# A two-block transformer stack in fp32: three edits at the start, at the bias rows and at the end

## The chip, the cores and the metric

The kernel runs on one core of one Trainium2 chip. The metric is device microseconds (us) of one execution; lower is better. The kernel before took 1858.72 us (median of 3 runs, 1858.06 to 1859.34).

## The reference

256 tokens of width 2048 go through two residual blocks and a norm, and then through a third block with two residual steps, all in fp32:

```
x = x + (mla(rmsnorm(x) @ w_in) * silu(gate)) @ w_out        # latent attention; c_q and c_kv are normed again
x = x + (swa(rmsnorm(x) @ w_in) * silu(gate)) @ w_out        # sliding window, 32 query heads
x = rmsnorm(x) * final_norm
proj = rmsnorm(x) @ w_in_2                                   # q, k, v of attention; z, xbc, dt of a state-space mixer
x = x + rmsnorm(concat(attn(q, k, v, rel_bias), ssm(z, xbc, dt)) @ w_out_2)
gate, up = split(causal_conv(rmsnorm(x) @ w_ffn_up))
x = x + rmsnorm((gelu(gate) * up) @ w_ffn_down)
```

The attention's relative bias depends on the head and on the distance of two tokens alone. In the latent attention `c_q` and `c_kv` (512 each) are columns of `rmsnorm(x) @ w_in` and get a norm of their own.

## The kernel before

Activations lie transposed: a tile `x` holds 128 features by 256 tokens, so the width is 16 tiles. The weights are a stream of some 600 pieces of 128 x 1024 fp32 (512 KB), in the order of use. `fetch` (L285 to 288) issues one on SyncE's queue (SP) into one of five buffers `raw`. `split_w` makes two halves of it: ScalarE copies it into the rounded type fp32r (`whi`, L304, told as L276 in the profile, since a helper records it), VectorE subtracts to get the rest (`wlo`, L305, told as L270); there are four buffers of each. Activations are split in the same way into one tile `hl` with the two halves side by side. In `proj` TensorE then multiplies `whi` by both halves (512 columns, L336) and `wlo` by the high half (256 columns, L339): one such pair per 128 features, eight pairs a piece, two pieces for one tile of 128 outputs in PSUM (`acc`). The two column halves of `acc` are added on the way out.

A scheduler sets the order of the instructions on each engine from its own estimate of their times; only parts marked `manual_schedule` keep the written order on the engines named there. All DMAs share eight completion lanes in rotation, so an engine that issues one can first have to wait for the one eight issues earlier. An engine that issues a DMA runs its instructions in order: what stands behind a waiting issue waits too.

The places that the change touches, in the order of the program:

- `start` (L652) issues the first loads on SP: x in groups of four tiles between half pieces of the first four weight pieces, and runs 14 small fp32 matmuls on a tile of ones (L662). `first_two` (L393) splits x times the layer's gain and the first four pieces in 256-column steps, in written order, and makes the first two output tiles side by side (L434, L437): 16 rows k, two accumulators each. Behind that the squares of x are summed for the first norm (`sq`, L421), and the norm `r1` is multiplied into each of the eight latent tiles `u` before their own norm.
- `out_mla` (L808) makes 16 output tiles with `proj`, two pieces each. At tile 8 it calls `biases` (L695): a matmul with a table of 0 and 1 spreads the relative bias over 384 distances for 8 heads, and one DMA on ScalarE's queue (L712) writes that row 128 times into DRAM (`biasrows`, 1536 KB), from where the attention later reads it skewed.
- `out_swa` (L906) makes 16 tiles and their norm; `mix` then begins with small preparations for the state-space part (L981 to 1000, L1013, L1032 to 1039): `wdts`, a 16-column weight in both halves, the exponential `ea`, scaled convolution weights, zeroed pads. The first matmuls of that stage (L351) multiply all 16 activations by `wdts`.
- `ffn` (L1213): the down projection turns the operands round, so that its outputs have 128 tokens by 512 columns. It has two passes `p` of 1024 outputs, 44 pieces each, and four accumulators (token half t, column half c). Token half 1 runs behind half 0 by `lag` pieces, and in the last pass its last four pieces are held to the end (`held`, L1268). Then come the final norm and the output, on VectorE in written order (L1310 to 1325): squares on ScalarE (`end`), the gain (`gain`), the sum and root, and eight outputs of 128 x 512, each with its DMA.

Of the kernel before, what the change touches and what calls it, by code (L numbers as in the profile page):

```python
# [40 lines left out]


class _Lazy:


    def __init__(self, n, make):
        self.n, self.make, self.made = n, make, {}

    def __len__(self):
        return self.n  # L50

    def __getitem__(self, k):
        if k not in self.made:
            self.made[k] = self.make(k)
        return self.made[k]
# [156 lines left out]

def _host(inputs):
    i = {n: np.asarray(a) for n, a in inputs.items()}
    return {
        "xt": np.ascontiguousarray(i["x"][0].T.reshape(KT, 128, S).transpose(1, 0, 2)),
# [11 lines left out]
class _Kernel:  # L228
    def __init__(self, ctx, tc, xt, pos, wst, wdt, vec, cst, rel, gfpost, out, dbg=None):
# [11 lines left out]
        self.raw = []  # L241
# [33 lines left out]
    def act(self, out, in_, func=AF.Copy, **kw):  # L275
        self.nc.scalar.activation(out, in_, func, **kw)  # L276
# [13 lines left out]
    def weights(self, pool=None):  # L290
        if not self.raw:
            self.fetch()
        self.piece += 1
        return self.split_w(self.raw.pop(0), HALF, pool)
# [98 lines left out]
    def first_two(self, xs, P):  # L393


        ws = []
        for i in range(4):
            self.piece += 1
            ws.append([self.wpool.tile([128, HALF], F32R, name=n, bufs=4) for n in ("whi", "wlo")])
        raw, self.raw = self.raw[:4], self.raw[4:]  # L400
        E = mybir.EngineType
        with self.tc.manual_schedule(engines={E.Activation, E.DVE}):
            for g in range(4):
                for k in range(4 * g, 4 * g + (2 if g == 0 else 4)):
                    xs[k]
                for i in (g // 2, 2 + g // 2):
                    hi, lo = ws[i]
                    for a in range(512 * (g % 2), 512 * (g % 2) + 512, 256):
                        w = slice(a, a + 256)
                        self.act(hi[:, w], raw[i][:, w])  # L410
                        self.tt(lo[:, w], raw[i][:, w], hi[:, w].bitcast(F32), ALU.subtract)
                if g == 0:
                    xs[2], xs[3]
            accs = self.columns(xs, ws)
            sums = []
            for x in self.x0:
                for a in (0, 2):
                    t = P.tile([128, 2, S], F32, name="sq2", bufs=4)
                    self.act(t, x[:, a : a + 2, :], AF.Square)
# [3 lines left out]
            t = sums[0]  # L423
            self.tt(t[:, 0, :], t[:, 0, :], t[:, 1, :], ALU.add)
# [78 lines left out]
    def rstd(self, c, n, out=None):  # L503
# [4 lines left out]
        self.act(r, c, AF.Sqrt, scale=1.0 / n, bias=self.eps)  # L508
        v.tensor_scalar(x, c, 1.0 / n, EPS, op0=ALU.mult, op1=ALU.add)
# [142 lines left out]
    def start(self):  # L652
# [4 lines left out]
        g1 = P.tile([128, KT], F32, name="g1")  # L657
        nc.scalar.dma_start(out=g1, in_=self.vec_dram[:, 0:KT])
        self.act(self.tmp("n0", (128, 2), 4), self.ones[:, 0:2])
        warm = self.aux.tile([128, 512], F32, name="s", bufs=2)  # L660
        for i in range(14):
            nc.tensor.matmul(warm[:, :128], self.ones, self.ones, start=True, stop=True)  # L662

        x4 = [P.tile([128, 4, S], F32, name="x0", bufs=4) for _ in range(4)]
        x0 = [t[:, j, :] for t in x4 for j in range(4)]
        self.raw = [self.new_raw() for _ in range(4)]
        self.fetched = 4
        for g in range(4):
            for a in (0, 2) if g == 0 else (0,):
                b = a + 2 if g == 0 else 4  # L670
                nc.sync.dma_start(out=x4[g][:, a:b, :], in_=self.xt[:, 4 * g + a : 4 * g + b, :])
                if a == 0:
                    w = slice(512 * (g % 2), 512 * (g % 2) + 512)
                    for i in (g // 2, 2 + g // 2):
                        nc.sync.dma_start(out=self.raw[i][:, w], in_=self.wst[i, :, w])
# [3 lines left out]
        self.x0 = x4  # L679
        self.xs = _Lazy(KT, lambda k: self.split(self.hx, 16, x0[k], g1[:, k : k + 1]))  # L680
# [14 lines left out]
    def biases(self, P):  # L695
# [5 lines left out]
        nc.scalar.dma_start(out=hot, in_=self.cst_dram[0:33, at : at + n])  # L701
        rel = P.tile([33, 8], F32, name="rel")
        nc.vector.memset(rel, NEG)
        nc.scalar.dma_start(out=rel[0:32, :], in_=self.rel)
# [5 lines left out]
        nc.scalar.dma_start(out=self.wdt, in_=self.wdt_dram)  # L710
        self.bias = self.tc.dram_tile([128, 8, n], F32, name="biasrows")
        nc.scalar.dma_start(out=self.bias.rearrange("i h n -> h i n"),  # L712
                            in_=row.unsqueeze(1).to_broadcast([8, 128, n]))

    def mla(self):
# [5 lines left out]
        with self.pool("latent", side="right") as P:  # L721
            lat = []
            with self.pool("squares") as Q:
                accs, t = self.first_two(xs, Q)
                self.r1 = self.spread(self.rstd(self.mean(t[:, 0, :]), D))
            for name, gain in (("q", "gq"), ("kv", "gkv")):
                hl, ss = [], None
                for j in range(4):
                    u = self.both(accs.pop(0) if accs else self.proj(xs))
                    self.tt(u, u, self.r1, ALU.mult)  # L730
# [3 lines left out]
                self.rstd(self.mean(ss), 512, c)  # L734
# [73 lines left out]
    def out_mla(self):  # L808
# [3 lines left out]
        with self.pool("again") as P:  # L812
            for j in range(KT):
                if j == 8:
                    self.biases(P)
                if j == KT - 1:
                    self.roots(self.x[-2])
                if j % 4 == 0:
                    x0 = P.tile([128, 4, S], F32, name="x0", bufs=2)
                    nc.sync.dma_start(out=x0, in_=self.xt[:, j : j + 4, :])  # L820
# [85 lines left out]
    def out_swa(self):  # L906
# [3 lines left out]
        old, self.x, self.xs, ss, sg = self.x, [], [], None, None  # L910
        for j in range(KT):
# [452 lines left out]
```

## Time and profile before

| | |
|---|---|
| median of 3 runs | 1858.72 us |
| profiled execution, its span | 1858.8 us, 1857.0 us |
| TensorE matmul busy | 1828.4 us, 98% |
| VectorE, ScalarE busy | 1398.4 us (75%), 1030.2 us (55%) |
| weight stream | 320.49 MB, 50.4% of the time of 16 DMA engines |

The span is the time from the first to the last instruction that the hardware profiler recorded; the 1.8 us around it are launch and end. A busy TensorE is one that has a matmul in flight; matmuls overlap by some 0.1 to 0.15 us, so distances between starts tell more than durations. A gap is shown as an idle time with the instruction whose end released it.

### The profile page before, as it was taken

The numbers are of one execution on the slowest core, as the hardware profiler recorded it, in microseconds if no ns is written. First come the engines' busy times: TensorE is split into PE (matmuls) and PEld (weight loads), VectorE is DVE, ScalarE is ACT, GpSimd is POOL, SyncE is SP. The second block draws the span as 40 slices with busy tenths as digits, with TensorE's granted clock in tenths as the row PEclk, the third lists the DMA queues.
The fourth block names the chain that finished last, engine by engine and source line by source line (L and its number), as shares of the span: only waits on it lengthen the run. The fifth ranks groups of instructions, "written<-read, shape, count | busy, mean of one in ns | idle before, by whom it ended". The sixth has DMA issues, their size and how long they took to land.

```text
span 1857.0 us, 27806 instructions
## 1 busy us (share of the span) xinstructions
PE 1828.4 (98%) x10306; PEld 1572.9 (85%) x10306; DVE 1398.4 (75%) x2578; ACT 1030.2 (55%) x1832; POOL 0.2 (0%) x4
## 2 busy tenths in 40 slices
PE   9999999999999999999999989999999999999997
PEld 8999987898888887888888878888888888888886
DVE  8887776787888677977766578888888888855554
ACT  8655554567777655556554565444444444544543
POOL 0000000000000000000000000000000000000000
PEclk9999999999999999999999999999999999999999
DMA  8544456654444454544454645555555555555553
GB/s 291 176 151 157 148 175 184 215 183 150 144 158 150 158 191 138 182 170 152 149 194 140 206 145 174 181 182 190 184 187 188 184 191 182 196 186 187 202 187 120
DMA packets 92556, 326.13 MB, mean 176 GB/s; under 512 B 10339, under 2 KB 12804, under 8 KB 92420
## 3 DMA queue, kind: packets, MB, share of 16 engines
q1 hardware_dynamic: 89568, 320.49, 50.4%
q10 hardware_dynamic: 2852, 3.86, 1.1%
q8 instruction: 81, 1.33, 0.3%
q14 instruction: 55, 0.45, 0.1%
HBM read 320.64 MB, written 3.67 MB: 175 GB/s over the span
## 4 chain that ended last, share of the span: by engine, by line
PE 94%; DMA 2%; DVE 2%; ACT 1%; issue 1%; SPq 0%; DVEq 0%; ACTq 0%
PE acc L336 44%; PE acc L339 23%; PE acc L1264 4%; PE acc L1265 4%; PE acc L1266 4%; DMA biasrows<-bias 2%; PE acc L469 1%; PE acc L470 1%; PE acc L468 1%; PE m L594 1%; PE acc L450 1%; PE acc L451 1%; PE acc L449 1%; PE m L582 1%; PE s L791 1%
## 5 line engine op out<-in xcount | busy, mean ns | idle before, releaser
L336 PE MATMUL acc<-hl,whi 128*128 128x512 f32 x3584 | 1279.3, 398 | 4.1 <-ACT whi L276 4.1
L339 PE MATMUL acc<-hl,wlo 128*128 128x256 f32 x3584 | 1016.5, 284 | 3.7 <-DVE wlo L270 3.7
L276 ACT ACTIVATE whi<-raw 128x1024 fp32r<-128x1024 f32 (+1 forms) x606 | 628.6, 1041 | 670.3 <-PE acc L336 311.8
L270 DVE TENSOR_TENSOR wlo<-raw,whi 128x1024 fp32r<-128x1024 f32 (+1 forms) x606 | 727.0, 1203 | 352.5 <-ACT whi L276 348.8
L336 PEld LDWEIGHTS acc<-hl,whi 128*128 128x128 f32 x3584 | 674.1, 188 | 161.0 <-ACT whi L276 6.0
L339 PEld LDWEIGHTS acc<-hl,wlo 128*128 128x128 f32 x3584 | 673.8, 188 | 11.8 <-DVE wlo L270 5.2
L1265 PE MATMUL acc<-wlo,hl 128*128 128x512 f32 x344 | 136.1, 397 | 0.0
L1266 PE MATMUL acc<-whi,hl 128*128 128x512 f32 x344 | 135.3, 394 | 0.0
L1264 PE MATMUL acc<-whi,hl 128*128 128x512 f32 x344 | 118.2, 396 | 0.0
L273 DVE SCALAR_TENSOR_TENSOR g<-pad,vec,g 128x256 f32<-128x256 f32 x176 | 84.2, 482 | 2.8
L1265 PEld LDWEIGHTS acc<-wlo,hl 128*128 128x128 f32 x344 | 64.7, 188 | 16.0
L1264 PEld LDWEIGHTS acc<-whi,hl 128*128 128x128 f32 x344 | 64.7, 188 | 15.6
L1266 PEld LDWEIGHTS acc<-whi,hl 128*128 128x128 f32 x344 | 64.7, 188 | 15.2
L270 DVE TENSOR_TENSOR u<-acc,u 128x256 f32<-128x256 f32 x182 | 75.7, 418 | 0.4
L276 ACT ACTIVATE u<-acc 128x256 f32<-128x256 f32 x184 | 67.2, 366 | 5.7 <-DVE q L270 2.8
L276 ACT ACTIVATE t<-t,nm 128x128 f32<-128x128 f32 x112 | 49.4, 444 | 2.3 <-DVE nm L545 1.4
L270 DVE TENSOR_TENSOR t<-s,cst 128x384 f32<-128x384 f32 (+1 forms) x64 | 32.8, 520 | 20.0 <-PE s L890 12.8
L469 PE MATMUL acc<-wlo,hl 128*128 128x512 f32 (+1 forms) x128 | 47.1, 368 | 0.0
L470 PE MATMUL acc<-whi,hl 128*128 128x512 f32 (+1 forms) x128 | 47.1, 368 | 0.0
L468 PE MATMUL acc<-whi,hl 128*128 128x512 f32 (+1 forms) x128 | 46.8, 368 | 0.0
L451 PE MATMUL acc<-hl,wlo 128*128 128x256 f32 x160 | 45.7, 285 | 0.0
L449 PE MATMUL acc<-hl,whi 128*128 128x256 f32 x160 | 45.5, 284 | 0.0
(294 smaller groups left out, 1652.7 us busy)
## 6 DMA issues: line engine op xcount, KB each, us to landing
raw<-in_wst_dram SPq DMA_DIRECT2D x593, 512.0 KB, 3.3
x<-in_xt_dram SPq DMA_DIRECT2D x7, 512.0 KB, 6.0
raw<-in_wst_dram SPq DMA_DIRECT2D x8, 256.0 KB, 6.1
biasrows<-bias ACTq DMA_DIRECT2D x1, 1536.0 KB
b<-biasrows ACTq DMA_DIRECT2D x8, 128.0 KB, 2.8
gb<-in_gfpost_dram ACTq DMA_DIRECT2D x2, 512.0 KB, 4.7
out_dram<-f SPq DMA_DIRECT2D x4, 256.0 KB, 2.3
out_dram<-hl SPq DMA_DIRECT2D x4, 256.0 KB, 2.5
```

Source lines behind the costliest of these rows:

```text
L270: self.nc.vector.tensor_tensor(out=out, in0=a, in1=b, op=op)
L273: self.nc.vector.scalar_tensor_tensor(out=out, in0=a, scalar=s, in1=b, op0=op0, op1=op1)
L276: self.nc.scalar.activation(out, in_, func, **kw)
L336: nc.tensor.matmul(acc.rearrange("p a t -> p (a t)"), hi[:, a : a + 128], xs[k].rearrange("p a t -> p (a t)"), start=(k == 0), stop=False, ...
L339: nc.tensor.matmul(acc[:, 0, :], lo[:, a : a + 128], xs[k][:, 0, :], start=False, stop=(k == n - 1), skip_group_check=True)
L451: nc.tensor.matmul(acc[:, 0, :], lo[:, a : a + 128], x[:, 0, :], start=False, stop=(k == 3))
L468: nc.tensor.matmul(o, xh, hi[:, a : a + n], start=(k == 0), stop=False)
L469: nc.tensor.matmul(o, xh, lo[:, a : a + n], start=False, stop=False)
L470: nc.tensor.matmul(o, xl, hi[:, a : a + n], start=False, stop=(k == last))
L1264: nc.tensor.matmul(o, xh, hi[:, w], start=(k == 0), stop=False)
L1265: nc.tensor.matmul(o, xh, lo[:, w], start=False, stop=False)
L1266: nc.tensor.matmul(o, xl, hi[:, w], start=False, stop=(k == NF - 1))
```

## The change

Three edits are joined.

1. Start. x is stored with its gain in front (`_pack_x`), so that no separate load of the gain is needed. The first loads go out on two queues: four quarter pieces on ScalarE's, x and the rest on SP's. The first eight rows of the first two output tiles are computed as 16 plain fp32 matmuls of 256 columns, unsplit weights by x times gain (`xg`); the halves of these eight x, which later pieces need, are made by a VectorE copy and a GpSimd subtraction. Rows 8 to 15 go in halves as before, in 512-column steps. The halves of the next two pieces follow directly (`halved`), and the squares are released behind them (`issue_after(self.begun)`). Seven warm-up matmuls stand instead of 14. `r1` is no longer multiplied into the latent tiles, but into the mean of their squares (twice) and their norm (once).
2. Bias rows. `biases` runs at tile 3 and writes one row of 12 KB (`biasrow`); tiles 4 to 11 each issue one DMA inside DRAM that copies this row into 16 of the 128 rows.
3. The state-space preparations move into `out_swa` (`ssm_ready`, at tile 5). In the last pass of the down projection six pieces of token half 1 are held instead of four and come last in order; the end runs by token half: two gains, the sum of the first three squares with the epsilon, the root with the last square added in ScalarE's bias, four outputs; the output (t=1, q=2) goes out on ScalarE's queue.

```diff
@@ first_two
+        xg = [self.wpool.tile([128, 4, S], F32, name=n, bufs=4) for n in ("whi", "wlo")]
...
+        def halves(k):
+            v = xg[k // 4][:, k % 4, :]
+            nc.vector.tensor_copy(xs[k][:, 0, :], v)
+            nc.gpsimd.tensor_tensor(out=xs[k][:, 1, :], in0=v, in1=xs[k][:, 0, :].bitcast(F32),
+                                    op=ALU.subtract)
...
+            for g in range(2):
+                for k in range(4 * g, 4 * g + 4):
+                    self.act(xg[g][:, k % 4, :], x(k), scale=gain(k))
+                for k in range(4 * g, 4 * g + 4):
+                    halves(k)
+            for g in range(2):
+                w = slice(512 * g, 512 * g + 512)
+                for i in range(2):
+                    hi, lo = ws[i]
+                    self.act(hi[:, w], raw[2 * i + 1][:, w])
+                    self.tt(lo[:, w], raw[2 * i + 1][:, w], hi[:, w].bitcast(F32), ALU.subtract)
...
+            self.halved = [self.weights(), self.weights()]
+            self.begun = self.act(self.tmp("n5", (128, 1), 1), self.g1[:, 0:1]).ins
+        for k in range(KT):
+            a = (k % 8) * 128
+            for i, acc in enumerate(accs):
+                if k < 8:
+                    nc.tensor.matmul(acc[:, 0, :], raw[2 * i][:, a : a + 128], xg[k // 4][:, k % 4, :],
+                                     start=(k == 0), stop=False, skip_group_check=True)
+                    continue
...
@@ start
+        for w in (slice(0, 256), slice(256, 512)):
+            for i in (0, 2):
+                nc.scalar.dma_start(out=self.raw[i][:, w], in_=self.wst[i, :, w])
+        at = (0, KT + S, KT + 2 * S, KT + 4 * S)
+        for a, b in zip(at, at[1:]):
+            nc.sync.dma_start(out=first[:, a:b], in_=self.xt[:, a:b])
...
+        group(1)
+        for i in (0, 2):
+            part(i, 1, nc.sync)
+        for g in range(2):
+            group(2 + g)
+            for i in (1, 3):
+                part(i, g, nc.sync)
@@ biases, copies, out_mla
-        nc.scalar.dma_start(out=self.bias.rearrange("i h n -> h i n"),
-                            in_=row.unsqueeze(1).to_broadcast([8, 128, n]))
+        one = self.tc.dram_tile([8, n], F32, name="biasrow")
+        nc.scalar.dma_start(out=one, in_=row)
+        return one
+
+    def copies(self, one, r):
+        h, n = one.shape
+        self.nc.scalar.dma_start(
+            out=self.bias[16 * r : 16 * r + 16].rearrange("i h n -> i (h n)"),
+            in_=one.rearrange("h n -> (h n)").unsqueeze(0).to_broadcast([16, h * n]))
...
-                if j == 8:
-                    self.biases(P)
+                if j == 3:
+                    row = self.biases(P)
+                if 4 <= j < 12:
+                    self.copies(row, j - 4)
@@ mla
-                    self.tt(u, u, self.r1, ALU.mult)
...
+                self.tt(q, self.mean(ss), r1, ALU.mult)
+                self.tt(q, q, r1, ALU.mult)
+                self.rstd(q, 512, c)
+                self.tt(c, c, r1, ALU.mult)
@@ out_swa
+            if j == 5:
+                self.ssm_ready(R)
@@ ffn
-                held = 4 if p else lag
+                held = 6 if p else lag
...
-                for t, c in ((0, 0), (0, 1), (1, 0), (1, 1)):
-                    end(t, c)
-                gain(0, 0)
...
-                out(0, 2, r0)
-                out(0, 3, r0)
+                for t in range(2):
+                    end(t, 0)
+                    gain(t, 0)
+                    end(t, 1)
+                    gain(t, 1)
+                    r = root(t, base(t, 1))
+                    for q in range(4):
+                        out(t, q, r, nc.scalar if t and q == 2 else nc.sync)
```

Where instructions move, the order on an engine shows it. The rows are line, operation, output <- inputs, and the semaphores that the instruction waits for.

VectorE behind the splits of the first four pieces, before (`sq` are the sums of squares, the first `wlo` of 128x1024 is that of the fifth piece):

```order
L270 TENSOR_TENSOR wlo<-raw,whi 128x256 [waits DMAHW6_49,Activation_49]
L270 TENSOR_TENSOR wlo<-raw,whi 128x256 [waits Activation_49]
L270 TENSOR_TENSOR sq_291<-sq_291,sq_293 128x512 [waits Activation_49]
L270 TENSOR_TENSOR sq_291<-sq_291,sq_296 128x512 [waits DVE_49,Activation_49]
L270 TENSOR_TENSOR gfp<-vec 128x16 [waits DMAHW1_49]
L270 TENSOR_TENSOR sq_291<-sq_291,sq_299 128x512 [waits DVE_49,Activation_49]
L270 TENSOR_TENSOR wlo<-raw,whi 128x1024 [waits DMAHW7_49,PE_49,Activation_49]
L270 TENSOR_TENSOR u<-acc,u 128x256 [waits Activation_49]
L270 TENSOR_TENSOR sq_291<-sq_291,sq_302 128x512 [waits DVE_49,Activation_49]
```

And after (`hl` are halves of x, the two `wlo` of 128x1024 those of the fifth and sixth piece):

```order
L262 TENSOR_TENSOR wlo<-raw,whi 128x512 [waits DMAHW6_49,Activation_49]
L262 TENSOR_TENSOR wlo<-raw,whi 128x512 [waits DMAHW7_49,Activation_49]
L265 SCALAR_TENSOR_TENSOR hl<-x_85,xfirst,hl 128x256 [waits DMAHW5_49,Activation_49]
L265 SCALAR_TENSOR_TENSOR hl<-x_85,xfirst,hl 128x256 [waits Activation_49] x3
L262 TENSOR_TENSOR wlo<-raw,whi 128x1024 [waits DMAHW0_49,Activation_49]
L262 TENSOR_TENSOR gfp<-vec 128x16 [waits DMAHW2_49]
L262 TENSOR_TENSOR wlo<-raw,whi 128x1024 [waits PE_49,DMAHW3_49,Activation_49,Pool_49]
L262 TENSOR_TENSOR sq_264<-sq_264,sq_266 128x512 [waits Activation_49]
L262 TENSOR_TENSOR sq_264<-sq_264,sq_269 128x512 [waits DVE_49,Activation_49]
```

Three sums of squares stood ahead of the first whole `wlo`; now two whole `wlo` stand ahead of them. The second of these waits for GpSimd, since its buffer is the one of `xg`, which GpSimd reads.

ScalarE around the bias rows in `out_mla`, before:

```order
L276 ACTIVATE whi<-raw 128x1024 [waits DMAHW4_49,PE_49,Activation_49]
L276 ACTIVATE bias<-m 8x384 [waits PE_49]
L712 DMA biasrows<-bias 8x128x384 [waits DMAHW3_49,Activation_49]
L276 ACTIVATE whi<-raw 128x1024 [waits DMAHW7_49,PE_49]
L276 ACTIVATE whi<-raw 128x1024 [waits DMAHW0_49,PE_49]
L276 ACTIVATE hl<-x,vec 128x256 [waits DVE_49]
L276 ACTIVATE ss<-x 128x256
L276 ACTIVATE hl<-x,vec 128x256 [waits DVE_49]
L276 ACTIVATE sq<-x 128x256
```

And after (`whi` of 128x1024 is a weight piece; the names DMAHW are completion lanes; the issue of `biasrow` stands just ahead):

```order
L268 ACTIVATE whi<-raw 128x1024 [waits DMAHW1_49,PE_49]
L268 ACTIVATE whi<-raw 128x1024 [waits DMAHW2_49,PE_49]
L761 DMA biasrows<-biasrow 16x3072 [waits DMAHW7_49,DMAHW5_49]
L268 ACTIVATE hl<-x,vec 128x256 [waits DVE_49]
L268 ACTIVATE ss<-x 128x256
L761 DMA biasrows<-biasrow 16x3072 [waits DMAHW0_49]
L268 ACTIVATE hl<-x,vec 128x256 [waits DVE_49]
L268 ACTIVATE sq<-x 128x256
L268 ACTIVATE whi<-raw 128x1024 [waits DMAHW3_49,PE_49]
L761 DMA biasrows<-biasrow 16x3072 x2
L761 DMA biasrows<-biasrow 16x3072 [waits DMAHW4_49]
L268 ACTIVATE whi<-raw 128x1024 [waits PE_49]
```

One issue has become nine, over four weight pieces; the last three copies stand just behind these rows.

TensorE where the state-space stage begins, before (`wdts` is the small weight):

```order
L336 MATMUL acc<-hl,whi 128x512
L339 MATMUL acc<-hl,wlo 128x256
L351 MATMUL acc<-hl,wdts 48x512 [waits DVE_49,PE_49]
L351 MATMUL acc<-hl,wdts 48x512 x14
L336 MATMUL acc<-hl,whi 128x512 [waits PE_49]
L339 MATMUL acc<-hl,wlo 128x256
L336 MATMUL acc<-hl,whi 128x512
L339 MATMUL acc<-hl,wlo 128x256
L336 MATMUL acc<-hl,whi 128x512
L351 MATMUL acc<-hl,wdts 48x512 [waits DVE_49]
L498 MATMUL m<-ones,ss 128x1 [waits DVE_49]
```

And after:

```order
L330 MATMUL acc<-hl,whi 128x512
L333 MATMUL acc<-hl,wlo 128x256
L345 MATMUL acc<-hl,wdts 48x512 [waits PE_49]
L345 MATMUL acc<-hl,wdts 48x512 x12
L345 MATMUL acc<-hl,wdts 48x512 [waits DVE_49]
L330 MATMUL acc<-hl,whi 128x512 [waits PE_49]
L333 MATMUL acc<-hl,wlo 128x256
L330 MATMUL acc<-hl,whi 128x512
L333 MATMUL acc<-hl,wlo 128x256
L330 MATMUL acc<-hl,whi 128x512
L333 MATMUL acc<-hl,wlo 128x256
L345 MATMUL acc<-hl,wdts 48x512 [waits DVE_49]
```

The first of these matmuls no longer waits for VectorE, the fourteenth does, and the fifteenth stands three pairs later.

## Rows read from the trace of the kernel before

**Rows 1.** The page: busy us, share of the span, instructions of each engine.

```profile
PE 1828.4 (98%) x10306; PEld 1572.9 (85%) x10306; DVE 1398.4 (75%) x2578; ACT 1030.2 (55%) x1832; POOL 0.2 (0%) x4
```

**Rows 2.** TensorE's timeline, 299 to 321 us: start us, us, line, [idle before].

```profile
299.75 0.51 PE L336 MATMUL acc<-hl,whi 128*128 128x512 f32 x1 [2.93 <-ACT whi L276]
...
301.39 0.63 PE L336 MATMUL acc<-hl,whi 128*128 128x512 f32 x1
...
302.03 0.63 PE L336 MATMUL acc<-hl,whi 128*128 128x512 f32 x1
...
320.24 0.39 PE L339 MATMUL acc<-hl,wlo 128*128 128x256 f32 x1 [0.68 <-DVE wlo L270]
```

**Rows 3.** The chain of waits, 275 to 325 us: start us, us, what.

```profile
279.83 34.60 DMA biasrows<-bias
314.50 3.27 DMA raw<-in_wst_dram
```

**Rows 4.** DMA in 279 to 320 us: packets, MB, share; KB, us to landing.

```profile
q10 hardware_dynamic: 1032, 1.57, 28.2%
...
raw<-in_wst_dram SPq DMA_DIRECT2D x11, 512.0 KB, 13.1
```

**Rows 5.** The page's DMA issues: KB each, us to landing.

```profile
raw<-in_wst_dram SPq DMA_DIRECT2D x593, 512.0 KB, 3.3
```

**Rows 6.** TensorE's timeline, 1 to 23 us.

```profile
1.05 6.26 PE L662 MATMUL s<-ones 128*128 128x128 f32 x28 [1.05 <-DVE ones L252]
...
20.20 0.51 PE L336 MATMUL acc<-hl,whi 128*128 128x512 f32 x1 [0.37 <-ACT whi L276]
21.67 0.38 PE L339 MATMUL acc<-hl,wlo 128*128 128x256 f32 x1 [0.96 <-DVE wlo L270]
21.89 0.40 PE L336 MATMUL acc<-hl,whi 128*128 128x512 f32 x1
...
22.24 0.40 PE L336 MATMUL acc<-hl,whi 128*128 128x512 f32 x1
```

**Rows 7.** Busy time by stretch, last the granted clock, DMA share, GB/s.

```profile
300.00:320.00 20.00, 18.81 (x97) 15.89 (x96) 12.83 (x20) 9.66 (x15) 0.00 (x0) 0.91 0.64 193
...
700.00:720.00 20.00, 16.49 (x84) 12.37 (x83) 11.61 (x39) 11.05 (x19) 0.00 (x0) 0.91 0.29 96
```

**Rows 8.** TensorE's timeline, 702 to 712 us.

```profile
706.24 5.19 PE L351 MATMUL acc<-hl,wdts 128*48 128x512 f32 x15 [3.51 <-DVE wdts L270]
711.27 0.39 PE L336 MATMUL acc<-hl,whi 128*128 128x512 f32 x1
```

**Rows 9.** VectorE's timeline, 702 to 707 us.

```profile
705.68 0.41 DVE L270 TENSOR_TENSOR wdts<-wdt,wdts 128x256 fp32r<-128x256 f32 x1
```

**Rows 10.** VectorE's timeline, first 23 us.

```profile
16.52 1.42 DVE L270 TENSOR_TENSOR wlo<-raw,whi 128x256 fp32r<-128x256 f32 x4
...
20.39 1.22 DVE L270 TENSOR_TENSOR wlo<-raw,whi 128x1024 fp32r<-128x1024 f32 x1
```

**Rows 11.** ScalarE's timeline, first 21 us.

```profile
4.06 0.91 ACT L276 ACTIVATE hl<-x,g 128x256 fp32r<-128x256 f32 x2 [1.38 <-DMA g<-in_vec_dram]
```

**Rows 12.** TensorE's timeline at 1011 us: fp32 matmuls, two records each.

```profile
1011.04 0.59 PE L594 MATMUL m<-pt,vatt 128*128 128x256 f32 x2
1011.47 0.38 PE L596 MATMUL m<-pt,vatt 128*128 128x128 f32 x2
```

**Rows 13.** DMA issues from 5.0 to 5.5 us: KB each, us to landing.

```profile
raw<-in_wst_dram SPq DMA_DIRECT2D x1, 256.0 KB, 6.7
```

**Rows 14.** VectorE's timeline, the end.

```profile
1844.63 0.15 DVE L1296 TENSOR_REDUCE rend<-sums 128x1 f32<-128x4 f32 x1
...
1845.92 0.75 DVE L273 SCALAR_TENSOR_TENSOR f<-f,n,x 128x512 f32<-128x512 f32 x1
...
1847.92 0.69 DVE L270 TENSOR_TENSOR hl<-acc,gb 128x512 f32<-128x512 f32 x1
...
1850.68 2.73 DVE L273 SCALAR_TENSOR_TENSOR hl<-hl,n,x 128x512 f32<-128x512 f32 x4
```

More of the change, by code (lines that the diff above doesn't have):

```diff
@@ L1 @@
 import math
-from contextlib import ExitStack
+from contextlib import ExitStack, nullcontext
 import numpy as np
@@ L391, in several, with first_two @@
         return self.columns(xs, [self.weights(extra if i > 3 else None) for i in range(2 * n)])
[L393 to L399, printed above, removed]
-        raw, self.raw = self.raw[:4], self.raw[4:]
-        E = mybir.EngineType
[L402 to L406, printed above, removed]
-                    hi, lo = ws[i]
[L408 to L416, printed above, removed]
+    def first_two(self, P):
+        nc, xs = self.nc, self.xs
+        raw, self.raw = self.raw[:4], self.raw[4:]
+        self.piece += 4
+        accs = [self.acc.tile([128, 2, S], F32, name="acc", bufs=4) for _ in range(2)]
+        xg = [self.wpool.tile([128, 4, S], F32, name=n, bufs=4) for n in ("whi", "wlo")]
+        ws = [[self.wpool.tile([128, HALF], F32R, name=n, bufs=4) for n in ("whi", "wlo")]
+              for _ in range(2)]
+        x = lambda k: self.x0[k // 4][:, k % 4, :]
+        gain = lambda k: self.g1[:, k : k + 1]
+        def halves(k):
[3 more added lines that the diff above has]
+                                    op=ALU.subtract)
+        E = mybir.EngineType
+        with self.tc.manual_schedule(engines={E.Activation, E.DVE, E.Pool}):
+            for g in range(2):
[6 more added lines that the diff above has]
+                for i in range(2):
+                    hi, lo = ws[i]
+                    self.act(hi[:, w], raw[2 * i + 1][:, w])
+                    self.tt(lo[:, w], raw[2 * i + 1][:, w], hi[:, w].bitcast(F32), ALU.subtract)
+                for k in range(8 + 4 * g, 12 + 4 * g):
+                    self.act(xs[k][:, 0, :], x(k), scale=gain(k))
+                    self.stt(xs[k][:, 1, :], x(k), gain(k), xs[k][:, 0, :].bitcast(F32),
+                             ALU.mult, ALU.subtract)
+            self.halved = [self.weights(), self.weights()]
[8 more added lines that the diff above has]
+                hi, lo = ws[i]
+                nc.tensor.matmul(acc.rearrange("p a t -> p (a t)"), hi[:, a : a + 128],
+                                 xs[k].rearrange("p a t -> p (a t)"), start=False, stop=False,
+                                 skip_group_check=True)
+                nc.tensor.matmul(acc[:, 0, :], lo[:, a : a + 128], xs[k][:, 0, :], start=False,
+                                 stop=(k == KT - 1), skip_group_check=True)
+        sums = []
+        with self.tc.issue_after(self.begun):
+            for v in self.x0:
@@ L678, in start @@
         nc.sync.dma_start(out=self.vec, in_=self.vec_dram)
-        self.x0 = x4
-        self.xs = _Lazy(KT, lambda k: self.split(self.hx, 16, x0[k], g1[:, k : k + 1]))
+        self.x0, self.g1 = x4, first[:, :KT]
+        self.xs = [self.hx.tile([128, 2, S], F32R, name="hl", bufs=16) for _ in range(KT)]
     def turns(self, P, j):
@@ L1275, in ffn @@
                             if 0 <= k < NF - held * t:
-                                add(t, k, c)
-                for c in range(2):
-                    for k in range(NF - held, NF):
-                        add(1, k, c)
+                                last = add(t, k, c)
+                with self.tc.issue_after(last) if p else nullcontext():
+                    for c in range(2):
+                        for k in range(NF - held, NF):
+                            add(1, k, c)
                 def end(t, c):
```

152 lines of the change are left out of this document (76 added, 76 removed).

## The prediction

> **What bounds the kernel now.** I read the page first. TensorE is busy for 98% of the span [rows 1], so a part of the change can pay only in three ways: it shortens TensorE's instructions, closes a gap between them, or brings the last output nearer to the last matmul. The changed kernel has the same weight pieces and, but for the first rows, the same matmuls, so I went through TensorE's timeline for gaps and looked, for each, at what ended it. Three places matter: the start, 300 to 320 us, and 706 us; their rows stand below, each at its term. A fourth place is the tail, where TensorE has ended and VectorE's outputs still run. The other gaps stand in places whose order the change leaves alone; I leave them as they are.
>
> **The bias rows.** The gap of 2.93 us in [rows 2] is ended by ScalarE's weight copy. The chain of waits names what is behind it: a DMA `biasrows<-bias` of 34.60 us, and only then a weight piece [rows 3]. In that window the bias queue used 28.2% of all engines for 1032 packets, and a weight piece took 13.1 us to land instead of 3.3 [rows 4, 5]. 28.2% of 16 engines over 41 us is 185 engine-us, 0.18 us a packet. Spread over 16 engines this is 11.6 us, over eight it is 23 us. With the weights' own share beside it, 34.6 us fits eight engines (the source has eight rows) and not sixteen.
> The price on TensorE: 2.93 of gap; the first pair takes 301.39 − 299.75 = 1.64 instead of 0.35 (the spacing in [rows 6]), so 1.29; four pairs run 0.64 apart instead of 0.35, 4 x 0.29 = 1.16; and a gap of 0.68 at 320.24 [rows 2]. Sum 6.1. The slow pairs are TensorE at its lower level, 1.2 GHz: granted clock 0.91 in 300 to 320 us [rows 7], just behind the gap.
> The change writes a 12 KB row and then eight copies of 196 KB, each of 16 rows of 12,288 B. The bytes are the same 1.57 MB but the runs are eight times longer. The trace has no such copy. Bounds: as costly as now (185 engine-us on half the engines, gain 0), or as cheap per byte as the weights (1.57 MB is three pieces of 512 KB at 3.3 us each, spread over four pieces' time; all of 6.1 comes back). I take the cheap end, since the rows resemble weight packets in length. The new cost is on ScalarE: nine DMA issues instead of one, each able to wait for a completion lane. In the order, the copies' lanes are those that the next weight copies wait for anyway (their own waits vanish from the rows), and two weight copies stand before the first copy, so TensorE has two pieces in hand, over 5 us. Term: **−6.1** (0 to −6.4).
> The Trainium skill ("DMA: Bandwidth & Descriptors", "Why a DMA increments its semaphore by 16 and not by 1") says a DMA uses the largest number of engines up to 16 that divides the slowest dimension: eight for the old source, sixteen for a copy. By the rule the copies use all the engines, −6.1; were the number of engines not tied to that dimension, the 34.6 us would need another cause and the term would be nearer 0. The packets' row above bears the rule out.
>
> **The state-space weights.** At 706.24 TensorE has been idle 3.51 us for `wdts` from VectorE, and fifteen matmuls then take 711.27 − 706.24 = 5.03 us [rows 8]; at the 0.23 us that half of a pair costs they would take 3.5, so 1.5 more goes to the clock (0.91 in 700 to 720 us, [rows 7]). VectorE made `wdts` at 705.68 [rows 9], behind setup that the change moves to the fifth tile of the stage before. In the new order the first of these matmuls waits for TensorE alone. What is late next is the fourteenth normed row: in the new order its matmul waits for VectorE, with thirteen, 3.0 us, ahead of it, and the fifteenth stands three pairs further on. Moving adds nothing new: the same small instructions now lie in a stretch where VectorE has a quarter of its time free [rows 1]. Term: **−5.0**. If the fourteenth row is itself late, a gap of 1 to 2 us stays: −5.0 to −3.
>
> **The start.** Before, the fourth piece's halves hold TensorE: 0.37 idle at 20.20 and 0.96 at 21.67, and full speed from 21.89 [rows 6]. VectorE is the reason: it ends the first pieces' low halves at 16.52 + 1.42 = 17.94 and then adds squares until 20.39 [rows 10]. In the changed kernel the squares come later, the next two pieces' halves directly.
> Step by step: the first x lands by about 4.0, where the first scale starts now; plus 0.45 for a scale [rows 11]: matmuls from about 4.5. Sixteen fp32 matmuls of 256 columns cost 0.43 each at full clock [rows 12], 6.9; the warm-up ran at about 0.45 for 128 columns until 7.3 [rows 6], the lower level, so three fit before 7.3 and thirteen after: rows done near 12.9 (11.4 at full clock throughout, 18.2 at half). Row 8 needs the second half-pieces: they stand behind the same 3 MB as before, landing 5.1 + 6.7 = 11.8 and a little later for the second [rows 13]; ScalarE's and VectorE's halves of them end near 14.2. From there the last parts decide again: rows 12 to 15 begin near 17.35 and end near 20.15, eight pairs of 0.35. VectorE ends its last subtraction near 18.9, one microsecond later than before, but has the next low half at 20.1 instead of 21.6. So the second hi matmul of that piece stands at 20.5 instead of 21.89: −1.4. I take off 0.4 for small waits. The r1 products that go (eight of 0.36) and the small ones that come lie beside full TensorE work. Term: **−1.0** (−2.5 to +1.5, the upper end if the fp32 rows run at half clock to the end).
> Not in the trace: a subtraction on GpSimd. GpSimd has four records, 0.2 us in all [rows 1], so no row prices it; VectorE's like is 0.36 [rows 10], and I take up to ten times that as the far end. Begun at about 5.3, its eight must be over when the sixth piece's halves take over the buffers that it reads (in the order that `wlo` waits for GpSimd): TensorE wants them at 20.15 + 2.83 = 23.0, less 2 x 1.22 for its two halves [rows 10] 20.6. That leaves 15.3 us, 1.9 us each. I take them as hidden, being nearer to VectorE's row.
> The Trainium skill ("SBUF — State Buffer", "SBUF: two separate sides") speaks against this: a VectorE operation with two SBUF inputs and a GpSimd operation that reads SBUF lock each other out whole. No run here shows it yet; by it VectorE's subtractions would stand behind GpSimd's, a rival below.
>
> **The tail.** TensorE's end is fixed by its work. Before, the last gain runs at 1847.92, then the root, two outputs, and four more from 1850.68 to 1853.41 [rows 14]. After, the reduction no longer stands ahead of the gain (at most 0.15 earlier; I take 1847.85); 0.69 for the gain, then from the reduction to the first output 1.29 as at 1844.63 to 1845.92, plus one more small step of 0.19: first output at 1850.02. Four outputs take 2.73: end 1852.75, **−0.65**. Token half 0 has finished its outputs under the 36 held matmuls. Against it: with six pieces held, the last pieces are used by one half alone, 6 x 0.233 = 1.4 us a piece, near VectorE's 1.22 and half the distance of the pieces used by both, so with four buffers the last may come 0.4 late. Net **−0.25** (−1.5 to +1).
>
> **Sum.** The profiled execution is 1858.8 (span 1857.0), the median 1858.72; no correction. 1858.8 − 6.1 − 5.0 − 1.0 − 0.25 = 1846.45; **1846.4**.
>
> **Rivals.**
> A. The copies stay dear: they use as much engine time as now, or ScalarE stands on lanes. For it: ScalarE issues nine transfers in four pieces' time. Against: the lanes are those of pieces needed anyway. Gain there 0 to 3: 1849.5 to 1852.5.
> B. GpSimd and VectorE hold each other up at the start (the rule named above is this mechanism). Eight subtractions of VectorE's size held up once each by 0.36 are 2.9 us on VectorE, which was the bound: start +1.5 to +3: 1849 to 1850.5. Against: GpSimd's work falls where VectorE waits for landings.
> C. Slower: GpSimd's subtraction costs over 3.9 us. Then 5.3 + 8p passes 20.6 by more than 15.5, TensorE stands at the sixth piece, and without the start's gain 1847.4 + 15.5 is 1862.9. At 4.2 us it gives 1865.7. Against: it needs eleven times VectorE's price.
> D. The move does not do what it says: another wait (the last normed rows) takes the place of `wdts`. Then about 3 to 4 stays: 1849.4 to 1850.4. For it: the row needed there is made in the same stretch; against: thirteen matmuls stand before it.
>
> **How the numbers follow.** Forecast 0.68, A 0.13, B 0.09, C 0.03, D 0.07. A difference of 0.2% is 3.7 us, about what a measurement can tell. Slower (above 1862.4) is C plus a little for the unseen, 0.04; same (1855 to 1862.4) needs two rivals at once or a smaller C, 0.03; faster 0.93. Low end: every term at its best, −6.4 −5.0 −2.5 −1.5, is 1843.4; less 1.3 for the spread of the three runs before, 1842. High end, with A, B or D one at a time and the dearest part of A left out: 1851.5.
>
> **What would show it.** Each step by its gap: no gap over 1 us near 300, weight landings near 3.3 us beside the copies, no wait for `wdts`, the first piece behind the first two accumulators at full speed by 20.5, four outputs of token half 1 as VectorE's last work, ending 0.65 us nearer to TensorE's end than now. A wait of ScalarE on a copy, a GpSimd row over 1.9 us, or TensorE waiting on the held pieces would make it wrong.

## The result and the profile after

The changed kernel takes 1846.69 us (median of 6 runs, 1845.85 to 1847.32) against 1858.39 us for the kernel before beside it: ratio 0.9934, 95% interval 0.9923 to 0.9944, 11.7 us less. The forecast was 1846.4 us. Its profiled run has a span of 1845.1 us, 11.9 less than before.

TensorE's timeline, first 23 us (start us, us, line, shapes, count, idle before and releaser), answers to [rows 6]:

```profile
4.57 4.91 PE L431 MATMUL acc<-whi,raw 128*128 128x256 f32 x16 [0.16 <-ACT whi L268]
...
13.87 0.50 PE L435 MATMUL acc<-hl,whi 128*128 128x512 f32 x1 [0.94 <-DVE hl L265]
...
19.57 0.40 PE L330 MATMUL acc<-hl,whi 128*128 128x512 f32 x1
...
19.92 0.39 PE L330 MATMUL acc<-hl,whi 128*128 128x512 f32 x1
```

The fp32 rows end at 13.87 − 0.94 = 12.9. The fifth piece follows without a gap, and its second hi matmul, at 21.89 before, starts at 19.92: 2.0 us earlier.

DMA from 279 to 300 us (queue, packets, MB, share of 16 engines; then KB, us to landing), answers to [rows 4]:

```profile
q10 hardware_dynamic: 265, 1.58, 22.1%
...
raw<-in_wst_dram SPq DMA_DIRECT2D x9, 512.0 KB, 4.4
biasrows<-biasrow ACTq DMA_DIRECT2D x8, 192.0 KB, 5.5
```

The copies move the same bytes in 22.1% of 16 engines over 21 us, 74 engine-us instead of 185, and a weight piece lands in 4.4 us instead of 13.1. Of the gaps in [rows 2] nothing is left. What that is worth can be read from matmuls that do the same work in both kernels, here the last one ahead of the old gap and the one behind the last gap. In the kernel before:

```profile
296.54 0.28 PE L339 MATMUL acc<-hl,wlo 128*128 128x256 f32 x1
...
320.47 0.39 PE L336 MATMUL acc<-hl,whi 128*128 128x512 f32 x1
```

And in the changed kernel:

```profile
294.83 0.28 PE L333 MATMUL acc<-hl,wlo 128*128 128x256 f32 x1
...
312.25 0.40 PE L330 MATMUL acc<-hl,whi 128*128 128x512 f32 x1
```

The distance between the two kernels grows from 1.7 to 8.2 us, so the stage takes 6.5 us less.

TensorE at the state-space stage, answers to [rows 8], with the last matmul ahead of it:

```profile
693.33 0.28 PE L333 MATMUL acc<-hl,wlo 128*128 128x256 f32 x1
693.45 3.41 PE L345 MATMUL acc<-hl,wdts 128*48 128x512 f32 x14
696.70 0.39 PE L330 MATMUL acc<-hl,whi 128*128 128x512 f32 x1
```

There is no wait, and the fourteen matmuls take 3.25 us (granted clock 1.00). Before, the last matmul ahead of them was

```profile
702.45 0.28 PE L339 MATMUL acc<-hl,wlo 128*128 128x256 f32 x1
```

and the next weight piece starts at 711.27 [rows 8], 8.82 us later; after, it is 3.37 us from 693.33 to 696.70. With the fifteenth matmul (0.23), which stands later now, the place takes 8.82 − 3.37 − 0.23 = 5.2 us less.

But 130 us on, in the head loop of the same stage, TensorE has gaps where it had none (`s<-acs,pick` opens a head, L494 is part of a weight piece):

```profile
825.06 0.28 PE L1155 MATMUL s<-acs,pick 128*128 128x256 f32 x1
...
825.85 0.38 PE L1155 MATMUL s<-acs,pick 128*128 128x256 f32 x1
...
827.39 0.38 PE L1155 MATMUL s<-acs,pick 128*128 128x256 f32 x1 [0.34 <-ACT ce L268]
828.06 0.51 PE L494 MATMUL acc<-whi,hl 128*128 128x512 f32 x1 [0.29 <-DVE u L262]
```

Three heads stand in a row with no weight pieces between them; before, the openings stand singly among weight pieces (at 835.80 and 836.84) and the other matmuls of two heads follow (at 837.99). Summed from start to next start, the matmuls of all 16 heads take 14.4 us in this trace and 12.2 in that of before. The gaps shown are 0.6 of these 2.2 us; the rest is longer distances between the small matmuls.

The end, answers to [rows 14]. TensorE's last gap and its last matmul:

```profile
1823.67 0.50 PE L1336 MATMUL acc<-wlo,hl 128*128 128x512 f32 x1 [0.43 <-DVE wlo L262]
...
1835.67 0.39 PE L1337 MATMUL acc<-raw,hl 128*128 128x512 f32 x1
```

VectorE's timeline:

```profile
1836.82 0.69 DVE L262 TENSOR_TENSOR hl<-acc,gb 128x512 f32<-128x512 f32 x1 [2.78 <-ACT m L268]
...
1840.29 1.41 DVE L265 SCALAR_TENSOR_TENSOR hl<-hl,n,x 128x512 f32<-128x512 f32 x2
```

VectorE ends 1841.70 − 1835.67 = 6.03 us behind the start of the last matmul. Before, the last matmul is

```profile
1846.61 0.39 PE L1266 MATMUL acc<-raw,hl 128*128 128x512 f32 x1
```

and VectorE's end at 1853.41 is 6.80 behind it. From the last matmul to the end of the span it is 9.4 us instead of 10.4. Ahead of the last pieces the distance between the two kernels is 11.6 us, at the last matmul 10.9: the held pieces cost 0.7.

By the two traces, then: start −2.0, bias rows −6.5, preparations −5.2, head loop +2.2, held pieces +0.7, end −1.0. Together that is −11.8, against 11.9 of span. The sum leaves out smaller shifts, which nearly cancel: 0.3 us of the start is lost again by 60 us, some 0.8 is gained between the bias rows and the state-space stage, and some 0.6 is lost between 1060 and 1180 us.

### The profile page after: what moved, and what is told of

Its sections match the earlier page's. It is cut to its first block, busy times and chain, and to the rows that moved or that the text cites. A ratio compares the mean times of both kernels' runs of the same rounds, so it can differ in the third digit from the quotient of the medians.

```text
span 1845.1 us, 27777 instructions
## 1 busy us (share of the span) xinstructions
PE 1825.3 (99%) x10292; PEld 1571.4 (85%) x10292; DVE 1395.3 (76%) x2566; ACT 1025.4 (56%) x1819; POOL 6.0 (0%) x12
## 4 chain that ended last, share of the span: by engine, by line
PE 96%; DVE 2%; DMA 1%; ACT 0%; issue 0%; SPq 0%; DVEq 0%; ACTq 0%
PE acc L330 45%; PE acc L333 23%; PE acc L1337 4%; PE acc L1335 4%; PE acc L1336 4%; PE acc L494 1%; PE acc L496 1%; PE acc L495 1%; PE m L620 1%; DMA raw<-in_wst_dram 1%; PE acc L476 1%; PE acc L477 1%; PE acc L475 1%; PE m L608 1%; PE s L850 1%; DVE wlo L262 1%
## 5 line engine op out<-in xcount | busy, mean ns | idle before, releaser
L494 PE MATMUL acc<-whi,hl 128*128 128x512 f32 (+1 forms) x128 | 46.9, 369 | 0.3 <-DVE u L262 0.3
```

Of the source, the lines that this page charges most:

```text
L494: nc.tensor.matmul(o, xh, hi[:, a : a + n], start=(k == 0), stop=False)
```

## The experiments

The runs' noise is about ±2 us on a ratio, so each is read by its trace first and its time second. The changed kernel was timed again, in turn with two of them (eight rows from DRAM; five held pieces):

> The changed kernel itself once more, as the measure for the kernels that run beside it. Nothing is edited: 1846.7 to 1847.8 us, as in its first runs and as the three kernels that differed from it in nothing that cost time.

1847.78 us, ratio 0.9945 (0.9932 to 0.9957). The measures for what follows are 1846.7 to 1847.8, so the runs below that were expected at 1846.7 within 0.7 us and came to 1847.8 or 1847.9 are not told from the changed kernel. Its start shows how much one execution differs from another: here the second hi matmul of the fifth piece is at 20.73, in the eleven other runs with the new start between 19.76 and 21.03. Part of that is TensorE's pace. Here the records of the fp32 matmuls stand 0.43 us apart up to 10.7 us and 0.22 behind that, in the first run up to 6.9 us, though the profile gives a granted clock of 1.00 in both; so these rows end at 15.0 us here and at 12.9 there.

**The bias rows as before.** Edit: `biases` at tile 8 with the old DMA, no copies.

```diff
-        nc.scalar.dma_start(out=one, in_=row)
+        nc.scalar.dma_start(out=self.bias.rearrange("i h n -> h i n"),
+                            in_=row.unsqueeze(1).to_broadcast([8, 128, n]))
```

> The changed kernel with the bias rows written as before: at tile 8, one DMA from eight rows, 128 runs of 1536 B each. My theory (that DMA holds up the weight pieces and nothing else made the gap): 6.5 us slower than the changed kernel, near 1853.2 us, with a TensorE gap of about 3 us ended by ScalarE's weight copy near 292 us, slow pairs behind it, and weight pieces landing in about 13 us there. Rival (the gap goes because the stage in front of it is ordered differently): within 2 us of 1846.7, no such gap.

1853.88 us (0.9976, 0.9967 to 0.9985), 6.1 to 7.2 more. TensorE's gap and the DMA in 279 to 314 us:

```profile
298.01 0.51 PE L330 MATMUL acc<-hl,whi 128*128 128x512 f32 x1 [2.81 <-ACT whi L268]
```

```profile
q10 hardware_dynamic: 1032, 1.57, 33.1%
...
raw<-in_wst_dram SPq DMA_DIRECT2D x9, 512.0 KB, 15.1
```

The whole of the term is this DMA: by the trace, TensorE's last matmul stands 6.1 us later than in the changed kernel. The next four runs ask what in it was dear.

**One copy instead of eight.** Edit: `copies` is called once, at tile 4, and its one DMA writes all 128 rows (`[128, h * n]`).

> The changed kernel, but at tile 4 one DMA copies the 12 KB row into all 128 rows (1.57 MB in one issue) instead of eight of 16 rows each. Theory (what counts is how the bytes go over the engines, in long runs on all sixteen): the copy takes about the same 75 engine-us as the eight, weight pieces land a little later, TensorE shows no gap, 1846.7 within 0.7 us. Rival (the splitting in eight issues is what spares the weights): one long queue of copies ahead of the weight pieces, a gap of 1 to 3 us near 290 us, 1848 to 1850.

1847.89 us, no gap, the copy lands in 9.4 us. The splitting is not needed.

**Short runs.** Edit: the row with a pitch of 512 elements.

```diff
-        one = self.tc.dram_tile([8, n], F32, name="biasrow")
+        one = self.tc.dram_tile([8, 512], F32, name="biasrow")[:, :n]
```

> The changed kernel, but the row of 8 heads is kept with a pitch of 2048 B, so that each of the eight copies is 16 x 8 runs of 1536 B, as short as in the kernel before. Theory (eight engines instead of sixteen were the cause of the gap, the length of the runs was not): some 1024 packets, 0.18 us each, 183 engine-us as before but over sixteen engines, 11.4 us each; no gap, or one under 1 us: 1846.7 to 1847.7. Rival (short runs were the cause): a gap as in the kernel before, 1849.7 to 1853.

1847.77 us, no gap. DMA in 279 to 300 us:

```profile
q10 hardware_dynamic: 1163, 1.58, 24.8%
```

24.8% x 16 x 21 / 1163 = 0.07 us a packet (0.08 for the packets of 1536 B alone), where I had expected 0.18: runs of 1536 B are cheap. The length was not the cause, but the reason given for it (same price over twice the engines) was wrong too.

**Eight rows, from DRAM.** Edit: the shape of the old DMA, from the DRAM row.

```diff
+            out=self.bias.rearrange("i h n -> h i n"),
+            in_=one.unsqueeze(1).to_broadcast([h, 128, n]))
```

> The changed kernel, but at tile 4 one DMA writes all 128 rows with the shape of the kernel before, eight rows outermost, 1024 runs of 1536 B, only from the row in DRAM instead of from SBUF. Theory of the prediction (a DMA from eight rows uses eight engines, and that makes the gap): 0.18 us a packet on half the engines, weight pieces landing in 10 us or more, a gap of 1 to 3 us, 1848 to 1853. Rival (reading each row from one SBUF partition made the packets slow): 0.07 us a packet as with the short runs, 84 engine-us over eight engines, 10.5 us; no gap over 0.5 us, 1846.7 to 1847.8.

1847.13 us, no gap near 290. In 279 to 300 us:

```profile
q10 hardware_dynamic: 1034, 1.57, 20.4%
...
raw<-in_wst_dram SPq DMA_DIRECT2D x7, 512.0 KB, 6.5
```

This is 0.066 us a packet. At most 11 of its packets overlap in the trace, against 19 in the run with short runs from sixteen rows, so it seems to go over fewer engines (the overlap is a rough count: 19 is more than the 16 that there are). It takes 18 us from the first packet to the last, and still nothing waits. The DMA is issued at 280.31 us, that of the first experiment at 278.21, so both meet the same part of the weight stream. The theory of the prediction falls, the rival stands: the dear thing was the source in SBUF.

**Sixteen rows, from SBUF.** Edit: the eight rows twice in SBUF, each of 16 partitions writing every second copy, otherwise the kernel of the first experiment.

```diff
+        nc.scalar.dma_start(out=self.bias.rearrange("(i c) h n -> (c h) i n", c=2),
+                            in_=row.unsqueeze(1).to_broadcast([16, 64, n]))
```

> The kernel of e1 (the bias rows written from SBUF at tile 8 in one DMA), but the eight rows stand twice in SBUF, in 16 partitions, and each of the 16 writes every second copy: 16 rows outermost, 64 runs of 1536 B each. Eight rows from DRAM cost 0.07 us a packet and made no gap, eight from SBUF 0.18 and made one; this run asks whether the gap needs both, the dear packet and the eight engines. Theory (the price belongs to packets whose source is in SBUF, and the gap to 185 engine-us on eight engines): still 0.18 us a packet and 185 engine-us, but on sixteen engines, over in half the time; weight pieces land in 5 to 9 us, gap under 1 us, 1847 to 1849.5. Rival (the price comes from eight engines at once on few SBUF rows or grows with more of them, so that the whole lasts as long): landing 13 us or more, a gap near 3 us, 1852 to 1854. A third way: the packet gets cheap, 0.1 us or less, with twice the rows: 1847.

1852.74 us (0.9972, 0.9962 to 0.9983). TensorE's gap, and the DMA in 279 to 297 us:

```profile
297.89 0.50 PE L330 MATMUL acc<-hl,whi 128*128 128x512 f32 x1 [2.60 <-ACT whi L268]
```

```profile
q10 hardware_dynamic: 1040, 1.57, 78.8%
q1 hardware_dynamic: 292, 1.09, 14.8%
...
raw<-in_wst_dram SPq DMA_DIRECT2D x5, 512.0 KB, 15.8
```

My theory missed: a packet costs 78.8% x 16 x 18 / 1040 = 0.22 us, sixteen engines finish in half the time, but for those 17 us the weights hardly move (14.8%), and the gap is nearly as long. The rival's result came, though not all of its mechanism: the price grew, but the whole did not last as long.

Why a packet from SBUF costs three times one from DRAM was not settled. The two runs from SBUF narrow it down: eight rows moved the 1.57 MB in 33.6 us (47 GB/s), sixteen in 16.8 (94 GB/s), the same 5.9 GB/s for each row. A limit at the source that goes with the number of SBUF rows would give this, with packets that wait there and hold the engines meanwhile. Rows and engines doubled together, so these two runs alone do not tell one from the other; but from DRAM eight rows took 18 us, so engines alone were not the limit. A source spread over more SBUF rows was not run.

**The preparations back in place.** Edit: `self.ssm_ready(P)` at the start of `mix`.

> The changed kernel with the state-space preparations back at the start of the mixing stage. My theory: the wait for wdts costs 5.2 us, but the order of the head loop falls back to that of before, in which its matmuls stand in larger groups and cost 2.1 us less; net 3.1 us slower than the changed kernel, near 1849.8, with the head loop's matmuls at 12.2 us by distance of starts instead of 14.4. Rival (the move is worth all that the wait cost, and the 2.1 us are lost for another reason that stays): 5.2 slower, near 1851.9, head loop still at 14.4.

1850.48 us (0.9954, 0.9942 to 0.9967), 2.7 to 3.8 more. The wait is back, and the matmuls of the heads take 12.2 us:

```profile
697.18 5.14 PE L345 MATMUL acc<-hl,wdts 128*48 128x512 f32 x15 [3.48 <-DVE wdts L262]
```

So the move is worth 5.2 us at its place, and its new order costs 2.2 further on.

**Heads in pairs.** Edit: the two heads of a pair share one tile `ce` and one product; the six products of the pair (`made`) are written behind it.

```diff
-                    self.act(ce, a[:, 128:256], AF.Exp)
-                    self.tt(ce, ce, bc[2 + g][:, 128:256], ALU.mult)
+                    self.act(ce[:, e, :], a[:, 128:256], AF.Exp)
+                    made.append((h, slice(64 * e, 64 * e + 64), m, ce[:, e, :]))
+                self.tt(ce, ce, bc[2 + g][:, 128:256].unsqueeze(1).to_broadcast([128, 2, 128]),
+                        ALU.mult)
+                for h, rr, m, c2 in made:
```

> The changed kernel with one edit in the state-space head loop: the two heads of a pair share one tile ce and one product with bc, and their six matmuls a chunk are written behind both. The scheduler then orders the heads in whole pairs, as in the kernel before; in the changed kernel three heads stand in a row and others are split. Theory (the 2.1 us that the head loop lost are due to that order): head loop near 12.3 us instead of 14.4, 1844.6. Rival (VectorE sets the pace there, and TensorE's earlier start can't be used): 1846.7 within 0.5, gaps elsewhere in the stage.

1845.09 us (0.9933, 0.9921 to 0.9946), a span of 1842.8. The heads take 12.6 us, and the gaps among them are gone. The order's theory holds: two heads, weight pieces, two heads:

```profile
825.18 0.28 PE L1155 MATMUL s<-acs,pick 128*128 128x256 f32 x1
...
825.97 0.38 PE L1155 MATMUL s<-acs,pick 128*128 128x256 f32 x1
...
832.09 0.28 PE L1155 MATMUL s<-acs,pick 128*128 128x256 f32 x1
```

The edit also makes one VectorE product of two (0.42 us instead of twice 0.28), which this run doesn't separate from the order; the run before it has all the products, the old order and 12.2 us.

**The start as before.** Edit: the kernel before with parts 2 and 3 of the change.

> The kernel before with the bias copies, the moved preparations and the new end, but the old start (14 warm-up matmuls, all 16 rows in halves, r1 multiplied into the latents). By the two traces the new start is worth 2.0 us at the fifth piece and loses 0.4 of it in the latents: 1.6 us slower than the changed kernel, near 1848.3. Rival (the start's gain is an accident of one profile, or all given back before the next stage): within 0.5 us of 1846.7.

1848.22 us (0.9945, 0.9933 to 0.9958): by time not to be told from the changed kernel. By the trace the second hi matmul of the fifth piece is back at 22.08, 1.0 to 2.3 us behind the runs with the new start. The lead of the changed kernel's first trace over this one does not last: it is 2.2 us at 22 us, 1.9 at 100, 1.3 at 500 and 0.7 at TensorE's last matmul (1835.67 against 1836.33). So the gain at its place is shown, and how much of it reaches the end is not.

**Halves on VectorE.** Edit: `self.tt` for `nc.gpsimd.tensor_tensor`.

> The changed kernel with the eight low halves at the start subtracted on VectorE instead of GpSimd (0.36 us each instead of 0.72). Theory (VectorE waits there for weight parts to land, so it matters little who subtracts): 1846.7 within 0.7 us, eight matmul pairs from about 13.9 us as now; the copies next to them at 0.3 us instead of 0.57. Rival (VectorE is the bound at the start): the pairs begin up to 2.9 us later, 1847.7 to 1849.6.

1847.75 us, pairs from 14.10 us. VectorE's groups from 4 to 11 us (count, busy us, mean ns), here and in the changed kernel, and GpSimd's there from 4 to 13 us:

```profile
L262 DVE TENSOR_TENSOR hl<-wlo,hl 128x256 fp32r<-128x256 f32 x4 | 1.7, 426 | 0.1
...
L403 DVE CAST hl<-wlo 128x256 fp32r<-128x256 f32 x4 | 1.2, 288 | 0.2 <-ACT wlo L268 0.2
```

```profile
L403 DVE CAST hl<-wlo 128x256 fp32r<-128x256 f32 x4 | 2.3, 608 | 0.4 <-ACT wlo L268 0.4
```

```profile
L404 POOL TENSOR_TENSOR hl<-wlo,hl 128x256 fp32r<-128x256 f32 x4 | 2.9, 750 | 0.2 <-DVE hl L403 0.2
```

Beside GpSimd a copy on VectorE takes twice as long, 608 ns instead of 288, and each copy that starts during a subtraction of GpSimd's ends 0.15 us behind it. Of the 3.4 us of subtractions that GpSimd takes over, 1.9 are given back in the copies (all eight: 4.3 us instead of 2.4). It costs nothing, since VectorE then waits for weights to land.

**The old end, and five held pieces.** Edits: the old order and four held pieces; then five held pieces with the new order and the paired heads.

> The changed kernel with four held pieces and the old written order of the end. By the two traces the new end saves 1.0 us behind TensorE's last matmul and pays about 0.6 in TensorE at the held pieces: 0.3 to 0.4 us slower than the changed kernel, near 1847.0, no TensorE gap in the last 30 us. Rival (the new end is worth its whole 1.0): 1847.7.

1847.91 us (0.9944, 0.9931 to 0.9956), not to be told apart by time. There is no gap at the held pieces, and it is 10.4 us from the last matmul to the end: by the traces the six held pieces cost 0.7 us and the new end gives 1.0, so that they nearly cancel.

> The changed kernel with the paired ce of the state-space heads and five held pieces instead of six in the last pass. The pair is worth 2.3 us of span. Theory (six held pieces cost 0.6 us in TensorE at the last weights, and five leave the outputs of token half 0 just enough time): no gap, or one under 0.2 us, ahead of the held matmuls, last output as close behind TensorE as with six: 1.8 to 2.9 us faster than the changed kernel on this chip. Rival (the last weights come as late with five, or the outputs of half 0 hold up the gain of half 1): 1.5 to 2.3 faster.

1845.34 us (0.9931, 0.9919 to 0.9944), 2.4 less than the changed kernel beside it. No gap ahead of the held matmuls; the end, TensorE's last matmul and VectorE's last gain:

```profile
1834.37 0.40 PE L1339 MATMUL acc<-raw,hl 128*128 128x512 f32 x1
```

```profile
1835.53 0.69 DVE L262 TENSOR_TENSOR hl<-acc,gb 128x512 f32<-128x512 f32 x1 [1.38 <-ACT m L268]
```

The gain follows 1.16 us behind, as with six. By the trace, then, five held pieces keep the end and drop the gap. This and the paired heads alone are the fastest kernels here; their intervals overlap that of the changed kernel, so that they are faster rests on the traces. The times of the two do not show a gain of five pieces over six.

## Why the prediction was right

- **Bias rows**, −6.1 forecast: 6.5 by the trace, 6.1 to 7.2 by the first experiment. The gap, the slow pairs and their price were read rightly, and rival A did not come: while ScalarE issues the copies it is never idle for more than 0.6 us, and the weight pieces landed in 4.4 us beside the copies (3.3 forecast) with no wait behind them. What failed is the reason for taking the cheap end, "since the rows resemble weight packets in length", and with it the weight put on eight engines: short runs are cheap too, and eight rows make no gap, when they come from DRAM. The row that held the answer, 0.18 us a packet of 1536 B, was that of a source in SBUF. So the cheap end was reached by a property of the copies that the prediction did not name. The rule of the Trainium skill ("DMA: Bandwidth & Descriptors", "Why a DMA increments its semaphore by 16 and not by 1") agrees with the packets that overlap at once in the trace (8 of the old DMA, 17 with sixteen rows from SBUF), so that the old DMA used eight engines stands; but it did not decide.
- **Preparations**, −5.0 forecast: 5.2 at the place, and rival D did not come: the fourteenth row was in time. What failed is "moving adds nothing new". I read the order at the first wait and not behind it, where the scheduler, with TensorE early, set three heads in a row: +2.2. No rival had this.
- **Start**, −1.0 forecast: −2.0 at its place in the first trace, −0.9 to −2.1 over all twelve. In the first trace the matmuls begin at 4.57 (4.5 forecast), the fp32 rows are done at 12.9 (12.9) and the pairs begin at 13.87 (14.2). The 12.9 is in part luck: the forecast let the slow pace end at 7.3, and over the twelve traces it ends between 4.9 and 10.7 and the rows between 12.5 and 15.0. The step that failed is "the last parts decide again" at 17.35: they had landed, the eight pairs ran on at 16.78, and the 0.4 for small waits was not needed. "Lie beside full TensorE work" did not quite hold for the norms: 0.3 us was lost again by 60 us. GpSimd took 0.73 us a subtraction, between the bounds and far from the 1.9 at which it would cost. Rival B came in another form, and hidden: VectorE's subtractions begin at 12.06, when GpSimd's are over, but its copies stood beside them. The Trainium skill ("SBUF — State Buffer", "Who interferes with whom") names `cast` among what can take the port pair that VectorE shares with GpSimd, and the trace agrees: the copies beside GpSimd take 608 ns instead of 288.
- **End**, −0.25 net forecast: −0.77 for VectorE's end (−0.65 forecast), and a gap of 0.43 at the held pieces (+0.4 forecast), which with the slower matmuls beside it costs 0.7. To the end of the span it is −1.0, net −0.3. The 0.2 between VectorE's end and the span's may come from the second queue, on which one of the last outputs now goes out and which I had put at nothing; no run separates it.

The total came out within 0.3 us because start, bias rows, preparations and end were better by 1.0, 0.4, 0.2 and 0.1 and met a head loop that was worse by 2.2. What was forecast to go did go, at all four places; but the reason for the copies' price was wrong, the cost of the new order was not seen, and that the sum agrees better than its terms is luck.

## What to carry to other kernels

Where a broadcast of a few SBUF rows into DRAM runs beside a weight stream, try writing it once into DRAM and copying it from there; here that was worth 6 us. Read the price of a packet in the queue's row and ask which of source, length and engines makes it, since they can be changed one at a time. When a wait is taken away under a scheduler, read the new order to the end of the stage, not only at the wait: what it gives back stands there as split groups of small matmuls. At an end with pieces held back, hold no more than the outputs of the other half need.

## What the runs showed of the hardware

A DMA packet of 1536 B took 0.18 us from eight SBUF rows, 0.22 from sixteen and 0.066 from eight rows in DRAM. Out of SBUF the whole went at 5.9 GB/s a row with eight rows and with sixteen. While sixteen engines served the SBUF source, the weights' queue got 14.8% of the time of all engines. A copy of 128x256 fp32 on VectorE took 288 ns alone and 608 beside a GpSimd subtraction of 0.75 us. In the first microseconds the records of fp32 matmuls stood 0.43 us apart and then 0.22; the change came between 4.9 and 10.7 us in twelve traces of the same start.
